# A conditioned decoder layer on one core: the modulation's multiply-adds placed behind later weight splits on VectorE, and the rotary half-swap moved from TensorE to VectorE

## The chip, the core and the metric

One core of one Trainium2 chip runs the whole layer as one program. The metric is the device time of that core in microseconds (us); smaller is better. The engines are named as the profile names them: PE is TensorE, PEld its weight load, DVE is VectorE, ACT is ScalarE, SP is the engine that issues nearly every transfer.

## What is computed

256 tokens of width 2048 pass through one layer and a final norm, all in float32:

```
mods = silu(c) @ ada_w + ada_b          # 9 vectors of 2048: shift, scale and gate of three sublayers
x += 1/2 * gate1 * SwiGLU_1(mod(norm(x)))
x += gate2 * W_out( sig(gA)*UpA(GatedDeltaNet(h)) + sig(gB)*UpB(NSA(h)) ),  h = mod(norm(x))
x += 1/2 * gate3 * SwiGLU_2(mod(norm(x)))
y  = RMSNorm(x)
rope(x) = concat(x1*cos - x2*sin, x2*cos + x1*sin, rest)    # x1, x2: 16 rows each of a head's 128
```

The nine modulation vectors need the whole of `ada_w` (2048 x 18432, 151 MB) for one token's worth of arithmetic. They are products of one row vector, so the kernel does them on DVE as multiply-adds and not on PE.

## The kernel before, in words

**Weights and their split.** Activations lie transposed, 128 channels by 256 tokens a tile. A weight arrives in chunks of 128 x 1024 numbers (512 KB, `raw`, `wload` L157, or `block_load` L329), six buffers in all (`RB = 6`, tag `raw`). ACT rounds a chunk to its high half (`whi`, L171), DVE subtracts to get the low half (`wlo`, L172, or L343 in `block_rows`); three buffers each (`WB = 3`). A buffer of `raw` comes free with the `wlo` that reads it. For every 128 x 128 block `product` (L177) issues a matmul of the high half against 512 columns (high and low half of the activation, L181) and one of the low half against 256 columns (L183). A projection of 2048 inputs is two chunks and 16 such pairs.

**The modulation.** `ada_unit` (L223) handles 256 rows of `ada_w` for 1024 columns: two loads `adaraw` (L230), 512 KB each and from the same six `raw` buffers, and for each a multiply-add on DVE into `acc` (L232 for the first row block, L234 for the rest). After eight units PE transposes `acc` (L240) and DVE sums it into `modc` (L241, L242). `ada(n)` calls the next units between projections, at a pace that `paces` sets: 16 units over the first 22 projections of the first feed-forward block and 32 over the next 42 (L592), then 4 over 27, 20 over 20 and 24 over 36 projections of the mixer (L606), 16 in the second feed-forward block. The 36 last projections of the mixer's paces are the merge gates and the up-projections (L1107 to L1129), the "merge stage" below. The first two modulation vectors are made in `mods` (L421) with loads `sada` (L434) and multiply-adds L441, L443, beside the first gate and up products.

**What sets the order.** A tile framework gives each engine one instruction list. It may reorder what the source has in sequence: an instruction goes into its engine's list when the framework's own estimate says its inputs are there. On the chip each engine takes its list strictly in order. SP's list of loads has the source's order, so numbers of tiles such as `raw_15147` and `adaraw_15238` grow in the order of the transfer queue.

**The rotary swap.** `rope` (L979) copies a 128 x 256 tile, and multiplies the first 32 rows by a constant 32-row matrix `C_ROT` on PE (L982) to exchange the two halves of 16 rows with a sign. DVE multiplies the result, from PSUM, by the sines (L984), the rows themselves by the cosines (L985) and adds (L986). It runs for four key tiles (`attend_in`) and eight query tiles (`soft` in `attend`).

Of the kernel before, what the change touches and what calls it, by code (L numbers as in the profile page):

```python
# [18 lines left out]
F32 = mybir.dt.float32  # L19
# [8 lines left out]
P = 128  # L28
# [33 lines left out]
C_ID, C_ONE, C_TRI, C_UP, C_SUF, C_NEG, C_CAUS, C_ROT = [i * P for i in range(8)]  # L62
C_COS = C_ROT + 32
# [6 lines left out]
def float_consts():  # L70
# [11 lines left out]
    for m in range(16):  # L82
        c[16 + m, C_ROT + m] = -1.0
        c[m, C_ROT + 16 + m] = 1.0
# [5 lines left out]
    c[:16, C_SIN:C_SIN + S] = c[16:32, C_SIN:C_SIN + S] = np.sin(ang)  # L90
# [17 lines left out]
def trunk(tc, a, out, stage=99, dbg=None):  # L108
    nc = tc.nc
    ctx = ExitStack()  # L110
    with ctx:
# [44 lines left out]

        def wload(src, nk):  # L157
            raws = []
            for k0 in range(0, nk, 8):
                n = min(8, nk - k0)  # L160
                raw = wp.tile([P, 8, P], F32, tag="raw", name="raw", bufs=RB)
                nc.sync.dma_start(raw[:, :n], src[:, k0:k0 + n])
                raws.append((raw, n))
            return raws

        def wsplit(raws):
            parts = []
            for raw, n in raws:
# [3 lines left out]
                nc.vector.tensor_sub(lo[:, :n], raw[:, :n], hi[:, :n])  # L172
# [50 lines left out]
        def ada_unit(m, hf, k2, st):  # L223
            if k2 == 0:
                st["acc"] = wp.tile([P, HC], F32, tag="acc", name="acc", bufs=1)
            acc = st["acc"]
            for j in range(2):
                kt = 2 * k2 + j
                raw = wp.tile([P, HC], F32, tag="raw", name="adaraw", bufs=RB)
                nc.sync.dma_start(raw, a["ada_w"][kt * P:(kt + 1) * P, m * D + hf * HC:m * D + (hf + 1) * HC])  # L230
                if kt == 0:
                    nc.vector.tensor_scalar(acc, raw, cact[:, kt:kt + 1], None, op0=OP.mult)  # L232
                else:
                    nc.vector.scalar_tensor_tensor(acc, raw, cact[:, kt:kt + 1], acc, op0=OP.mult, op1=OP.add)  # L234
            if k2 == KT // 2 - 1:
                c0 = hf * 8
                for q in range(2):
                    pt = ftile((P, 4, P))
                    for j in range(4):
# [3 lines left out]
                                     V["ada_b"][:, m * KT + c0:m * KT + c0 + 8])  # L243

# [68 lines left out]
        def gains(A, gain, m_scale, sl):  # L313
            nc.vector.scalar_tensor_tensor(A[:, sl], modc[:, m_scale, sl], 1.0, gain[:, sl], op0=OP.add, op1=OP.mult)
            nc.vector.tensor_scalar(A[:, sl], A[:, sl], RS, None, op0=OP.mult)
# [22 lines left out]
        def block_rows(ps, srcs, hT, k0, kb, first, last):  # L338
# [4 lines left out]
            nc.vector.tensor_sub(lo, raw, hi)  # L343
# [9 lines left out]
        class Entry:  # L353
# [56 lines left out]
        def start(fp, n, sizes, wgu, gain):  # L410
# [9 lines left out]
            with tc.tile_pool(name="sp", bufs=1) as sp:  # L420
                def mods(k0, kb):  # L421
# [10 lines left out]
                    for kt in range(KT):  # L432
# [11 lines left out]
                        yield  # L444
                    sl = slice(k0, k0 + kb)
# [70 lines left out]
        def ffn(fp, wgu, wd, m_gate, ticks, first, post=None):  # L516
            if True:
# [21 lines left out]
                def down(g):  # L539
                    if g == 0:  # L540
                        nc.vector.tensor_scalar(g05, modc[:, m_gate], 0.5, None, op0=OP.mult)
# [62 lines left out]
        with ExitStack() as mx:  # L604
# [386 lines left out]
            def attend_in(g):  # L991
                kk = mp.tile([P, 2, S], F32, tag="kk", name="kk", bufs=2)
                vt = mp.tile([P, 2, 2, P], F32, tag="vt", name="vt", bufs=2)
                for b in range(2):
                    rope(both(win(W_KV + 4 * (b + 1) + g)), kk[:, b], ftile, tmp)
# [35 lines left out]
            def attend(g, kk, vt, qs):  # L1031
# [3 lines left out]
                def soft(r, qt):  # L1035
                    if qt == 0:
                        qr[r] = rope(qs[r], mp.tile([P, S], F32, tag="qr", name="qr", bufs=2), ptile, tmpc)
# [101 lines left out]
        g2 = nrm.tile([P, KT], F32, tag="g05", name="g05", bufs=2)  # L1139
        nc.vector.tensor_scalar(g2, modc[:, 5], 0.5, None, op0=OP.mult)  # L1140
# [100 lines left out]
```

## Time and profile before

| what | before |
|---|---|
| time, median of 3 runs | 2400.68 us (2399.38 to 2405.51) |
| profiled execution: its own time | 2402.11 us |
| profiled execution: span of the trace | 2400.3 us |
| PE busy | 2333.8 us, 97% of the span |
| DVE busy | 1786.4 us, 74% |
| ACT busy | 1130.7 us, 47% |
| moved by DMA | 571 MB, 238 GB/s over the span |
| share of the chain that ended last | PE 79%, DMA 9%, DVE 8% |

The span is counted from the first to the last instruction of the core; the profiled execution's own time is 1.8 us more. A busy time of PE is a model of overlapping matmuls, so the places where PE is idle, and the number of matmuls in equal stretches, say more than its busy share. Most rows of the profile give a line, an engine, an operation, what is written from what is read, a count, and times.

### The profile page before, as it was taken

What the parts mean: (1) busy time and instruction counts of PE and PEld (TensorE: products, weight loads), DVE (VectorE), ACT (ScalarE), POOL (GpSimd) and SP (SyncE); (2) the same over time, 40 slices, a digit from 0 to 9 for tenths busy, and PEclk for the clock granted to TensorE, in tenths of its full rate; (3) what the DMA queues carried; (4) which work ended last, traced back from release to release, by engine and by line L of the source; (5) the groups of instructions that cost most, each with busy time, mean ns of one, the idle gap of its engine ahead of it and who ended that gap; (6) DMA issues with size and microseconds to landing.
All of it is one profiled execution on the core that took longest, in us unless ns stands there. A gap on an engine that the chain in (4) does not pass through costs nothing.

```text
span 2400.3 us, 39307 instructions
## 1 busy us (share of the span) xinstructions
PE 2333.8 (97%) x15310; PEld 2048.3 (85%) x15310; DVE 1786.4 (74%) x2637; ACT 1130.7 (47%) x1784; POOL 1.5 (0%) x8
## 2 busy tenths in 40 slices
PE   6999999999999999999999989999999999999997
PEld 6999978888888988888887878889888888888886
DVE  6899878778887887789886777888666666555555
ACT  3544544334444565554444434556444444344443
POOL 0000000000000000000000000000000000000000
PEclk8999999999999999999999999999999999999999
DMA  9998688888887645558676877666777776665663
GB/s 326 321 318 308 202 280 302 282 279 295 315 306 221 221 164 189 185 178 270 223 241 222 293 266 241 208 229 195 237 239 237 239 239 197 185 191 187 181 185 122
DMA packets 182827, 571.05 MB, mean 238 GB/s; under 512 B 18032, under 2 KB 18288, under 8 KB 182640
## 3 DMA queue, kind: packets, MB, share of 16 engines
q1 hardware_dynamic: 181920, 566.43, 72.2%
q8 instruction: 120, 1.97, 0.3%
q10 hardware_dynamic: 720, 2.11, 0.2%
q14 instruction: 67, 0.55, 0.1%
HBM read 564.27 MB, written 4.19 MB: 237 GB/s over the span
## 4 chain that ended last, share of the span: by engine, by line
PE 79%; DMA 9%; DVE 8%; issue 2%; ACT 1%; DVEq 0%; SPq 0%; ACTq 0%
PE mm L181 41%; PE mm L183 21%; PE mm L348 9%; DMA adaraw<-in_ada_w_dram 8%; DVE wlo L172 3%; PE c L348 2%; DMA sada<-in_ada_w_dram 1%; DVE acc L234 1%; DVE sacc L443 1%; DVE wlo L343 1%; DMA raw<-in_win_dram 0%; PE c L1041 0%; PE f L240 0%; ACT whi L171 0%; PE c L817 0%
## 5 line engine op out<-in xcount | busy, mean ns | idle before, releaser
L181 PE MATMUL mm<-hpair,whi 128*128 128x512 f32 x3536 | 1259.5, 398 | 1.4 <-ACT t L203 1.4
L172 DVE TENSOR_TENSOR wlo<-raw,whi 128x1024 fp32r<-128x1024 f32 (+1 forms) x666 | 792.9, 1196 | 347.0 <-ACT whi L171 345.7
L171 ACT ACTIVATE whi<-raw 128x1024 fp32r<-128x1024 f32 (+1 forms) x666 | 689.8, 1037 | 760.2 <-PE mm L181 449.0
L183 PE MATMUL mm<-hpair,wlo 128*128 128x256 f32 x3536 | 1003.7, 284 | 21.3 <-DVE wlo L172 21.1
L181 PEld LDWEIGHTS mm<-hpair,whi 128*128 128x128 f32 x3536 | 665.1, 188 | 159.4 <-issue 2.8
L183 PEld LDWEIGHTS mm<-hpair,wlo 128*128 128x128 f32 x3536 | 668.3, 189 | 33.3 <-DVE wlo L172 28.1
L181 PE MATMUL mm<-apair,whi 128*128 128x512 f32 x1408 | 498.1, 397 | 0.0
L183 PE MATMUL mm<-apair,wlo 128*128 128x256 f32 x1408 | 397.2, 282 | 3.3 <-DVE wlo L172 3.1
L234 DVE SCALAR_TENSOR_TENSOR acc<-adaraw,cact,acc 128x1024 f32<-128x1024 f32 x210 | 269.0, 1281 | 133.2 <-DMA adaraw<-in_ada_w_dram 132.1
L181 PEld LDWEIGHTS mm<-apair,whi 128*128 128x128 f32 x1408 | 264.3, 188 | 64.6
L183 PEld LDWEIGHTS mm<-apair,wlo 128*128 128x128 f32 x1408 | 265.4, 188 | 5.5 <-DVE wlo L172 5.5
L348 PE MATMUL mm<-hpair,whi 128*128 128x256 f32 x1472 | 265.0, 283 | 2.4 <-ACT hpair L309 1.8
L348 PEld LDWEIGHTS mm<-hpair,whi 128*128 128x128 f32 x1472 | 227.9, 190 | 3.0 <-ACT hpair L309 1.9
L348 PE MATMUL mm<-hpair,wlo 128*128 128x256 f32 x736 | 208.2, 283 | 0.5 <-DVE wlo L343 0.4
L342 ACT ACTIVATE whi<-raw 128x1024 fp32r<-128x1024 f32 x112 | 118.5, 1059 | 144.5 <-DMA raw<-in_w1gu_dram 53.6
L343 DVE TENSOR_TENSOR wlo<-raw,whi 128x1024 fp32r<-128x1024 f32 x112 | 136.4, 1222 | 29.2 <-ACT whi L342 29.0
L348 PEld LDWEIGHTS mm<-hpair,wlo 128*128 128x128 f32 x736 | 139.6, 190 | 1.1 <-DVE wlo L343 1.0
L207 ACT ACTIVATE t<-mm 128x256 f32<-128x256 f32 x237 | 86.4, 366 | 0.1
L210 DVE TENSOR_TENSOR t<-mm,t 128x256 f32<-128x256 f32 x193 | 80.7, 418 | 2.9 <-ACT t L207 2.8
L443 DVE SCALAR_TENSOR_TENSOR sacc<-sada,cact,sacc 128x1024 f32<-128x1024 f32 x57 | 73.0, 1281 | 5.9 <-DMA sada<-in_ada_w_dram 5.5
L532 ACT ACTIVATE t<-t 128x256 f32<-128x256 f32 x63 | 26.3, 418 | 98.4 <-DVE t L210 98.2
L546 DVE SCALAR_TENSOR_TENSOR xT<-mm,g,xT 128x256 f32<-128x256 f32 x128 | 61.7, 482 | 7.7 <-PE mm L183 5.6
(374 smaller groups left out, 1563.5 us busy)
## 6 DMA issues: line engine op xcount, KB each, us to landing
adaraw<-in_ada_w_dram SPq DMA_DIRECT2D x224, 512.0 KB, 5.0
raw<-in_w2gu_dram SPq DMA_DIRECT2D x180, 512.0 KB, 4.7
raw<-in_w1gu_dram SPq DMA_DIRECT2D x176, 512.0 KB, 5.7
raw<-in_win_dram SPq DMA_DIRECT2D x158, 512.0 KB, 5.0
sada<-in_ada_w_dram SPq DMA_DIRECT2D x64, 512.0 KB, 6.1
raw<-in_w1d_dram SPq DMA_DIRECT2D x64, 512.0 KB, 4.6
raw<-in_w2d_dram SPq DMA_DIRECT2D x64, 512.0 KB, 3.6
raw<-in_wup_dram SPq DMA_DIRECT2D x32, 512.0 KB, 4.6
```

The costliest lines, as they stand in the source:

```text
L171: nc.scalar.activation(hi[:, :n], raw[:, :n], AF.Copy)
L172: nc.vector.tensor_sub(lo[:, :n], raw[:, :n], hi[:, :n])
L181: nc.tensor.matmul(ps[:, :], hi, pairs[k][:, :, :].rearrange("p a b -> p (a b)"), start=(k == 0), stop=False, skip_group_check=True)
L183: nc.tensor.matmul(ps[:, S:2 * S], lo, pairs[k][:, 0, :], start=False, stop=(k == n - 1), skip_group_check=True)
L207: nc.scalar.activation(t, ps[:, S:2 * S], AF.Copy)
L210: nc.vector.tensor_add(o, ps[:, :S], t)
L234: nc.vector.scalar_tensor_tensor(acc, raw, cact[:, kt:kt + 1], acc, op0=OP.mult, op1=OP.add)
L342: nc.scalar.activation(hi, raw, AF.Copy)
L343: nc.vector.tensor_sub(lo, raw, hi)
L348: nc.tensor.matmul(ps[:, w], l[:, w, k], h[:, r], start=(first and w == k == x == 0), stop=(last and k == kb - 1 and x == 2), skip_group_c ...
L443: nc.vector.scalar_tensor_tensor(acc, raw, c, acc, op0=OP.mult, op1=OP.add)
L546: nc.vector.scalar_tensor_tensor(xT[:, d], pd[:, j * S:(j + 1) * S], g05[:, d:d + 1], xT[:, d], op0=OP.mult, op1=OP.add)
```

## The change

Two things are changed.

First, the multiply-adds of the modulation are no longer issued where their loads are. `ada_unit` and `mods` put them into a list `late`. Each low-half split (`wlo`, in `wsplit` and `block_rows`) then takes entries out of that list, all but one of them or the only one, and ties each to stand behind this `wlo` in DVE's instruction list. Since the loads of the following projection are issued after the modulation's, such a `wlo` reads a chunk that is later in the transfer queue than the multiply-add's own load. Before a use of the results `flush` empties the list. The loads themselves stay where they were.

Second, `rope` uses DVE's `stream_shuffle` within 32 rows in place of the matmul; the sign goes into the sine constants and the matrix `C_ROT` goes away.

```diff
-    for m in range(16):
-        c[16 + m, C_ROT + m] = -1.0
-        c[m, C_ROT + 16 + m] = 1.0
...
+        late = []
+
+        def behind(ins):
+            for _ in range(max(1, len(late) - 1) if late else 0):
+                with tc.issue_after(ins.ins):
+                    late.pop(0)()
+
+        def flush():
+            while late:
+                late.pop(0)()
...
-                nc.vector.tensor_sub(lo[:, :n], raw[:, :n], hi[:, :n])
+                behind(nc.vector.tensor_sub(lo[:, :n], raw[:, :n], hi[:, :n]))
...
         def ada_unit(m, hf, k2, st):
...
+            for kt in (2 * k2, 2 * k2 + 1):
+                raw = wp.tile([P, HC], F32, tag="raw", name="adaraw", bufs=RB)
+                nc.sync.dma_start(raw, a["ada_w"][kt * P:(kt + 1) * P, m * D + hf * HC:m * D + (hf + 1) * HC])
+                late.append(lambda kt=kt, raw=raw: add(kt, raw))
+            if k2 == KT // 2 - 1:
+                late.append(columns)
...
-            nc.vector.tensor_sub(lo, raw, hi)
+            behind(nc.vector.tensor_sub(lo, raw, hi))
...
                         elif kt == 0:
-                            nc.vector.tensor_scalar(acc, raw, c, None, op0=OP.mult)
+                            late.append(lambda raw=raw, c=c: nc.vector.tensor_scalar(acc, raw, c, None, op0=OP.mult))
                         else:
-                            nc.vector.scalar_tensor_tensor(acc, raw, c, acc, op0=OP.mult, op1=OP.add)
+                            late.append(lambda raw=raw, c=c: nc.vector.scalar_tensor_tensor(
+                                acc, raw, c, acc, op0=OP.mult, op1=OP.add))
+                        if k0 == 0:
+                            flush()
                         yield
+                    flush()
...
-            def rope(x, o, pt, tr):
+            def rope(x, o, tr):
                 nc.scalar.activation(o, x, AF.Copy)
-                pr = pt((P, S))
-                nc.tensor.matmul(pr[:32], cf[:, C_ROT:C_ROT + 32], x, start=True, stop=True)
                 t = tr()
-                nc.vector.tensor_mul(t[:32], pr[:32], cf[:32, C_SIN:C_SIN + S])
+                nc.vector.stream_shuffle(t[:32], x[:32], [(i + 16) % 32 for i in range(32)])
+                nc.vector.tensor_mul(t[:32], t[:32], cf[:32, C_SIN:C_SIN + S])
                 nc.vector.tensor_mul(o[:32], x[:32], cf[:32, C_COS:C_COS + S])
```

`flush()` also stands in `gains`, `shift`, `down(0)` and ahead of `g2`.

**The order on DVE in the merge stage, before.** This is DVE's list around the loads `raw_15145` to `adaraw_15241`; `cat`, `t` and `Dt` belong to the merge arithmetic, `modc` to the end of a modulation vector.

```order
L172 TENSOR_TENSOR wlo_15150<-raw_15145,whi_15149 128x1024
L210 TENSOR_TENSOR cat_14963<-mm_15012,t_15063 128x256
L241 TENSOR_REDUCE modc_77<-f_15091 128x4
L232 TENSOR_SCALAR acc_15237<-adaraw_15238,cact_68 128x1024
L242 TENSOR_TENSOR modc_77<-modc_77,vec_71 128x8
L234 SCALAR_TENSOR_TENSOR acc_15237<-adaraw_15241,cact_68,acc_15237 128x1024
L210 TENSOR_TENSOR t_15117<-mm_15098,t_15115 128x256
L172 TENSOR_TENSOR wlo_15154<-raw_15147,whi_15153 128x1024
L1125 SCALAR_TENSOR_TENSOR Dt_13932<-Dt_13932,t_15117 128x256
L172 TENSOR_TENSOR wlo_15198<-raw_15193,whi_15197 128x1024
```

The multiply-adds of `adaraw_15238` and `adaraw_15241` stand ahead of the splits of `raw_15147` and `raw_15193`, which are earlier in the transfer queue.

**The same place with the change.** The four loads of the merge gates are now `raw_15118` to `raw_15183`, the modulation's pair is `adaraw_15225` and `adaraw_15227`, and `raw_15233`, `raw_15235` are the next up-projection's.

```order
L183 TENSOR_TENSOR wlo_15186<-raw_15181,whi_15185 128x1024
L1148 TENSOR_TENSOR Dt_13917<-Dt_13917 128x256
L250 TENSOR_REDUCE modc_77<-f_15138 128x4
L183 TENSOR_TENSOR wlo_15190<-raw_15183,whi_15189 128x1024
L251 TENSOR_TENSOR modc_77<-modc_77,vec_71 128x8
L183 TENSOR_TENSOR wlo_15238<-raw_15233,whi_15237 128x1024
L221 TENSOR_TENSOR cat_15116<-mm_15117,t_15177 128x256
L238 TENSOR_SCALAR acc_15241<-adaraw_15225,cact_68 128x1024
L183 TENSOR_TENSOR wlo_15244<-raw_15235,whi_15243 128x1024
L241 SCALAR_TENSOR_TENSOR acc_15241<-adaraw_15227,cact_68,acc_15241 128x1024
```

The two multiply-adds moved behind all four earlier chunks and behind one and two chunks that come after them in the queue.

**The rotary swap.** On PE, before, this is the place in the first attention group where a key tile's swap (`f<-t,cf`) and a query tile's (`c<-q,cf`) stand among the matmuls of projections:

```order
L1043 MATMUL c<-cr 128x2x128
L982 MATMUL f<-t,cf 32x256
L183 MATMUL mm<-hpair,wlo 128x256
L181 MATMUL mm<-hpair,whi 128x512
L1065 MATMUL c<-cf,G 128x128 x2
L982 MATMUL c<-q,cf 32x256
L183 MATMUL mm<-hpair,wlo 128x256
```

With the change PE's list has none of the twelve L982, and DVE's has twelve shuffles; here are the first two query tiles' on DVE:

```order
L1005 STREAM_SHUFFLE tc<-q 32x256
L1007 TENSOR_TENSOR qr<-q,cf 32x256
L1006 TENSOR_TENSOR tc<-tc,cf 32x256
L1005 STREAM_SHUFFLE tc<-q 32x256
L1008 TENSOR_TENSOR qr<-qr,tc 32x256
L1006 TENSOR_TENSOR tc<-tc,cf 32x256
L1007 TENSOR_TENSOR qr<-q,cf 32x256
```

Four instructions of DVE per tile stand where there were three.

## Rows read from the trace of the kernel before

**Rows 1.** The page: the chain that ended last, share of the span by engine.
```profile
PE 79%; DMA 9%; DVE 8%; issue 2%; ACT 1%; DVEq 0%; SPq 0%; ACTq 0%
```

**Rows 2.** Stretches: us, busy (count) PE PEld DVE ACT POOL, clock, DMA share, GB/s.
```profile
37.00:300.00 263.00, 260.57 (x2159) 258.80 (x2160) 230.51 (x289) 126.50 (x172) 0.00 (x0) 0.98 0.84 286
300.00:450.00 150.00, 144.15 (x815) 123.75 (x814) 118.10 (x140) 65.42 (x96) 0.00 (x0) 1.00 0.87 292
450.00:600.00 150.00, 145.78 (x824) 125.15 (x823) 116.63 (x132) 57.84 (x65) 0.00 (x0) 1.00 0.86 284
600.00:800.00 200.00, 199.20 (x1131) 172.41 (x1130) 158.76 (x212) 95.15 (x134) 0.00 (x0) 1.00 0.83 280
...
1150.00:1250.00 100.00, 100.00 (x577) 81.84 (x576) 84.63 (x189) 48.85 (x115) 0.00 (x0) 1.00 0.69 224
1250.00:1350.00 100.00, 96.46 (x550) 82.20 (x549) 71.21 (x104) 46.34 (x78) 0.00 (x0) 1.00 0.75 247
1350.00:1450.00 100.00, 90.23 (x498) 76.83 (x497) 71.93 (x86) 41.01 (x56) 0.00 (x0) 0.98 0.80 269
1450.00:1500.00 50.00, 47.66 (x271) 40.93 (x271) 37.05 (x52) 23.27 (x37) 0.00 (x0) 1.00 0.75 242
...
1650.00:2380.00 730.00, 730.00 (x4199) 637.19 (x4198) 454.30 (x574) 345.35 (x480) 0.00 (x0) 1.00 0.66 206
```

**Rows 3.** Waits: who waited for whom, us in total, times, longest us.
```profile
DVE acc L234 <- DMA adaraw<-in_ada_w_dram: 132.1, 90, 4.5
...
PE mm L183 <- DVE wlo L172: 24.3, 25, 2.2
```

**Rows 4.** One stall, by engine: start us, us, engine, line, what [idle before].
```profile
1396.00 0.68 DVE L241 TENSOR_REDUCE modc<-f 128x4 f32<-128x512 f32 x1
1400.56 0.75 DVE L232 TENSOR_SCALAR acc<-adaraw,cact 128x1024 f32<-128x1024 f32 x1 [3.88 <-DMA adaraw<-in_ada_w_dram]
...
1403.35 1.22 DVE L172 TENSOR_TENSOR wlo<-raw,whi 128x1024 fp32r<-128x1024 f32 x1
...
1399.98 1.06 ACT L171 ACTIVATE whi<-raw 128x1024 fp32r<-128x1024 f32 x1 [1.48 <-issue]
...
1404.62 0.38 PE L183 MATMUL mm<-hpair,wlo 128*128 128x256 f32 x1 [1.54 <-DVE wlo L172]
```

**Rows 5.** SP's issues there: start of first, us to end of last, count.
```profile
1392.95 1.43 SPq L230 DMA_DIRECT2D adaraw<-in_ada_w_dram  x2
1395.78 5.89 SPq L162 DMA_DIRECT2D raw<-in_wup_dram  x2
```

**Rows 6.** The tile adaraw, issue to landing; the page's median landing of sada.
```profile
DMA to landing us min/median/max: 3.4/5.0/7.7
...
sada<-in_ada_w_dram SPq DMA_DIRECT2D x64, 512.0 KB, 6.1
```

**Rows 7.** Groups by line: count | busy us, mean ns | idle before, releaser.
```profile
L172 DVE TENSOR_TENSOR wlo<-raw,whi 128x1024 fp32r<-128x1024 f32 (+1 forms) x666 | 792.9, 1196 | 347.0 <-ACT whi L171 345.7
L171 ACT ACTIVATE whi<-raw 128x1024 fp32r<-128x1024 f32 (+1 forms) x666 | 689.8, 1037 | 760.2 <-PE mm L181 449.0
...
L234 DVE SCALAR_TENSOR_TENSOR acc<-adaraw,cact,acc 128x1024 f32<-128x1024 f32 x210 | 269.0, 1281 | 133.2 <-DMA adaraw<-in_ada_w_dram 132.1
...
L210 DVE TENSOR_TENSOR t<-mm,t 128x256 f32<-128x256 f32 x193 | 80.7, 418 | 2.9 <-ACT t L207 2.8
```

**Rows 8.** PE's list in time at one swap; L982 appears as two rows.
```profile
1157.64 0.62 PE L982 MATMUL c<-q,cf 128*32 128x256 f32 x2
1158.19 0.50 PE L181 MATMUL mm<-hpair,whi 128*128 128x512 f32 x1
```

**Rows 9.** Groups by line, nearest prices for a shuffle.
```profile
L798 DVE STREAM_TRANSPOSE tb<-zc 128x128 f32<-128x128 f32 x20 | 6.1, 306 | 0.3
...
L985 DVE TENSOR_TENSOR qr<-q,cf 32x256 f32<-32x256 f32 x8 | 3.2, 406 | 0.0
...
L896 DVE TENSOR_TENSOR o<-o,roy 128x512 f32<-128x512 f32 x4 | 2.7, 685 | 0.1
```

More of the change, by code (lines that the diff above doesn't have):

```diff
@@ L59 @@
 ROPE_DIM = 32
-C_ID, C_ONE, C_TRI, C_UP, C_SUF, C_NEG, C_CAUS, C_ROT = [i * P for i in range(8)]
-C_COS = C_ROT + 32
+C_ID, C_ONE, C_TRI, C_UP, C_SUF, C_NEG, C_CAUS = [i * P for i in range(7)]
+C_COS = C_CAUS + P
 C_SIN = C_COS + S
@@ L89, in float_consts @@
     c[:16, C_COS:C_COS + S] = c[16:32, C_COS:C_COS + S] = np.cos(ang)
-    c[:16, C_SIN:C_SIN + S] = c[16:32, C_SIN:C_SIN + S] = np.sin(ang)
+    c[16:32, C_SIN:C_SIN + S] = np.sin(ang)
+    c[:16, C_SIN:C_SIN + S] = -c[16:32, C_SIN:C_SIN + S]
     for qt in range(2):
@@ L223, in ada_unit, with add, columns @@
         def ada_unit(m, hf, k2, st):
[L224 to L230, printed above, removed]
+            def add(kt, raw):
                 if kt == 0:
-                    nc.vector.tensor_scalar(acc, raw, cact[:, kt:kt + 1], None, op0=OP.mult)
+                    st["acc"] = wp.tile([P, HC], F32, tag="acc", name="acc", bufs=1)
+                    nc.vector.tensor_scalar(st["acc"], raw, cact[:, kt:kt + 1], None, op0=OP.mult)
                 else:
+                    acc = st["acc"]
                     nc.vector.scalar_tensor_tensor(acc, raw, cact[:, kt:kt + 1], acc, op0=OP.mult, op1=OP.add)
-            if k2 == KT // 2 - 1:
+            def columns():
+                acc = st["acc"]
                 c0 = hf * 8
@@ L440, in mods @@
                         elif kt == 0:
-                            nc.vector.tensor_scalar(acc, raw, c, None, op0=OP.mult)
+                            late.append(lambda raw=raw, c=c: nc.vector.tensor_scalar(acc, raw, c, None, op0=OP.mult))
                         else:
-                            nc.vector.scalar_tensor_tensor(acc, raw, c, acc, op0=OP.mult, op1=OP.add)
+                            late.append(lambda raw=raw, c=c: nc.vector.scalar_tensor_tensor(
+                                acc, raw, c, acc, op0=OP.mult, op1=OP.add))
+                        if k0 == 0:
+                            flush()
                         yield
+                    flush()
                     sl = slice(k0, k0 + kb)
@@ L540, in down @@
                     if g == 0:
+                        flush()
                         nc.vector.tensor_scalar(g05, modc[:, m_gate], 0.5, None, op0=OP.mult)
@@ L994, in attend_in @@
                 for b in range(2):
-                    rope(both(win(W_KV + 4 * (b + 1) + g)), kk[:, b], ftile, tmp)
+                    rope(both(win(W_KV + 4 * (b + 1) + g)), kk[:, b], tmp)
                     v = both(win(W_KV + 4 * (b + 1) + 2 + g))
@@ L1036, in soft @@
                     if qt == 0:
-                        qr[r] = rope(qs[r], mp.tile([P, S], F32, tag="qr", name="qr", bufs=2), ptile, tmpc)
+                        qr[r] = rope(qs[r], mp.tile([P, S], F32, tag="qr", name="qr", bufs=2), tmpc)
                     n = (qt + 1) * P
@@ L1139, in trunk @@
         g2 = nrm.tile([P, KT], F32, tag="g05", name="g05", bufs=2)
+        flush()
         nc.vector.tensor_scalar(g2, modc[:, 5], 0.5, None, op0=OP.mult)
```

## The prediction

> **What bounds the kernel now.** I read the chain that ended last first. PE holds 79% of it, transfers 9% and DVE 8% [rows 1], so the kernel is PE's, with a fringe where PE waits for something that DVE and the transfer queue hand on. To see where that fringe lies I cut the span into stretches [rows 2]. From 1650 to 2380 us PE is never idle, and 730 us for 4199 matmuls is 0.174 us a matmul; a projection of 2048 inputs, 32 matmuls, costs 5.56 us at that pace. PE falls behind in two places. Between 300 and 800 us its idle time is 5.85 + 4.22 + 0.80 = 10.9 us, between 1250 and 1500 us it is 3.54 + 9.77 + 2.34 = 15.7 us. These are the stretches in which the modulation's loads run beside projections; where they are rare the idle time is gone.
>
> The table of waits names the link: PE waited 24.3 us in 25 places for a low half, and DVE waited 132.1 us in 90 places with a multiply-add at the head of its list for that multiply-add's load [rows 3]. One stall shows how the two hang together [rows 4]. DVE has nothing it may do from 1396.7 us on, because `adaraw` stands next in its list; that load lands only at 1400.5 us. ACT finished the high half of an earlier chunk at 1399.98 + 1.06 = 1401.04 us, but its low half waits behind two multiply-adds and starts at 1403.35 us, and PE stands idle until 1404.62 us. The stalled load itself was issued late [rows 5], and the second load of the next pair was issued when the first multiply-add was over (1400.56 + 0.75 = 1401.31 us; the issue ends at 1401.67 us, 0.4 us later): a buffer ring that is held up by its own newest loads.
>
> **The multiply-adds.** Their number and length don't change: 210 of 1.28 us and 14 short ones, on DVE, which has room. What changes is their place. By the list of before, 201 of the 224 stand ahead of one to five splits of chunks that are earlier in the queue; by the new list 222 stand behind every earlier chunk, and 221 behind one or two later ones as well. The loads keep their order on SP, so no transfer is moved past another, but the moment of each issue moves, since a buffer is released by another instruction.
>
> In the built programs I counted, for the merge stage, how many loads earlier the releasing instruction's own load is. Before: for 20 of 37 issues that wait for a multiply-add it is three loads, and for those that wait for a split six to ten. With the change: four to six for a split, seven or eight for a multiply-add. So the short loop of before is landing, multiply-add 1.28 us [rows 7], 0.4 us to the next issue: with the median landing of 5.0 us [rows 6] 6.7 us for three loads, 2.2 us a load. What PE asks for in the merge stage is 120 loads (48 + 72) for 36 projections, 120 in 36 x 5.56 = 200 us, 1.67 us a load. Three such loops stand for about ten loads, 20.1 us, where three projections take 16.7.
>
> The tight loop of the change is longer but spans more: issue, landing, high half 1.04, low half 1.20, an add 0.42, multiply-add 1.28, low half 1.20, multiply-add 1.28 [rows 7], 0.4 to the issue: landing + 6.8 us for six loads. The other four loads of three projections go at DVE's own pace, two splits, two multiply-adds and two adds, 5.8 us. Together landing + 12.6 us for ten loads: 17.6 us at a landing of 5.0 us, 16.6 us at 4.0 us, against PE's 16.7.
>
> How much of the 24.3 us goes follows from where that lies. The loop of before overstates: it gives 2.01 us a load at 5.0 us, while the stretch itself ran at 1.67 x 250 / 234.3 = 1.78 us. Scaled by the same factor the new loop gives 1.56 us, faster than PE, and all 24.3 us go; taken at face value it gives 1.76 us, and nothing goes. Those are the two ends. I take 70%, 17 us, nearer the first, because the new loop holds a landing once in ten loads and the old one three times, and because releases that alternate between splits and multiply-adds should spread the issues, which shortens the landing towards its shortest, 3.4 us [rows 6].
>
> The Trainium skill (DMA: Bandwidth & Descriptors, Anatomy of one DMA) puts one DMA at about 2.0 us plus its bytes over 436 GB/s, measured on the other issue path; that is an estimate of 3.2 us for 512 KB. The shortest landing in the trace, 3.4 us, agrees; the median does not, since loads queue behind each other. By the page's figure the new loop would take 15.8 us for ten loads and every wait would go.
>
> **The rotary swap.** Twelve matmuls of PE go, each two rows in the profile. From the start of such a pair to the start of the next matmul it is 1158.19 - 1157.64 = 0.55 us [rows 8], 6.6 us in all, in a part where PE is never idle (1150 to 1250 us, 100.00 of 100 us [rows 2]). On DVE twelve shuffles of 32 x 256 come in. No row has one: the nearest are 0.31 us for a transposing stream of 128 elements, 0.41 us for a two-operand product of this very tile, and 0.69 us for 512 elements [rows 9]. I take the row of this tile, 0.41 us, 4.9 us in all, between 3.7 and 8.2. They lie beside PE's work, but DVE is 84.6% busy there [rows 2]; with 4.9 us more in a stretch 6.6 us shorter it is at 96%, little cover. So I book 5 us of the 6.6, with 0 and 6.6 as ends.
>
> The Trainium skill (VectorE: DVE Perf Modes, The perf-mode tier table) gives the shuffle one element a cycle and no faster mode, about 2400 ns for 2048 elements. An estimate from that page, 150 cycles and 256 cycles at 0.96 GHz, is 0.42 us, or 5.1 us for twelve; no run here shows it.
>
> **The sum.** The profiled execution took 2402.1 us. Less 17 and 5 it is 2380.1; it lay 1.4 us above the median of the runs, so against the median I expect **2379 us**.
>
> **Rivals.**
>
> *Every wait goes.* By the scaled loop PE would never wait in these stretches and the swap would save its full 6.6 us: 2402.1 - 24.3 - 6.6 - 1.4 = 2370 us. For it speaks that from 600 to 800 us, at 280 GB/s, PE lost only 0.8 us [rows 2]. Against it: some places need ten loads in less than the loop's time. Chance 0.13.
>
> *The transfers are the limit.* At full pace the first feed-forward block's gate and up projections ask for 3.52 loads in 5.56 us, 332 GB/s; 292 GB/s went with a DMA share of 0.87 [rows 2], which is 336 at a full share. If that can't be reached nothing is won before 800 us: 2402.1 - 0.7 x 15.7 - 5 - 1.4 = 2385 us. Chance 0.07.
>
> *The wait changes its name.* A low half now waits for its own chunk, whose load is issued four to six loads after the one that releases its buffer, where it was six to ten. At face value the loop is as slow as now, and only the swap pays: 2402.1 - 5 - 1.4 = 2396 us. Chance 0.15, one third of it below 2393.5.
>
> *Slower: the first 300 us starve.* There the change touches a stretch in which PE loses only 263 - 260.6 = 2.4 us [rows 2]. A `raw` load's issue waits for a split five loads earlier (38 of 51), before six or seven. PE's 24 matmuls per chunk take 2.92 us (263 us / 2159 x 24) and ask for 1.9 loads, 1.54 us a load. The loop is landing 6.1 us [rows 6], 1.04 + 1.20 [rows 7] and 0.4: 8.7 us for five loads, 1.75 us. Over some 114 loads that is 0.21 x 114 = 24 us. If the later waits stay too, the time is 2402.1 + 24 - 5 - 1.4 = 2420 us. It decides from a landing above 5 x 1.54 - 2.64 = 5.1 us on. Against it: 6.1 us is the landing with more loads in flight, and a shorter ring shortens it. Chance 0.10.
>
> **How the numbers follow.** A measurement of this kernel can tell about 0.3%, 7 us, from no change: faster is below 2393.5, slower above 2407.9. The forecast, with 2372 to 2388 around it, has the 0.55 that is left. Faster: 0.55 + 0.13 + 0.07 + 0.05 = 0.80; same 0.10; slower 0.10. The range of 2368 to 2397 takes in all cases but the slower one and leaves out a little at either edge of the others, together under 0.2; it spans the two ends of both unknown costs.
>
> **What would show it.** In the changed profile DVE's wait for `adaraw` (132.1 us) should nearly vanish and its wait for the high half grow; PE's wait for the low half should fall from 24.3 to about 7 us; the stretch of the merge gates should lose its 15.7 us of idle time. L982 is gone, and twelve shuffles of about 0.4 us stand on DVE with PE still fully busy around them. The forecast is wrong if PE's wait for the low half stays over 15 us, if PE shows new idle time before 300 us, or if PE waits for query tiles in the attention.

## Result and profile after

| | before | change |
|---|---|---|
| time, median of the undisturbed runs | 2401.89 us (2399.38 to 2405.51) | 2424.44 us (2418.93 to 2434.23) |
| ratio, 95% interval | | 1.0099 [1.0074, 1.0123] |
| profiled execution: span, own time | 2400.3, 2402.11 us | 2422.6, 2424.44 us |
| PE busy, idle | 2333.8, 66.5 us | 2333.6, 89.0 us |

The change is 1% slower; 2379 us, 2368 to 2397, had been forecast. (A fourth run of the change, at a granted clock of 0.653, took 3224 us and is left out; with it the median is 2429 us, the number that the expectations below use.)

The chain that ended last has less of PE than in [rows 1], and its transfers are no longer `adaraw` (8% of the span on the page of before) but weight chunks:

```profile
PE 67%; DMA 15%; DVE 9%; ACT 4%; issue 3%; ACTq 0%; DVEq 0%; SPq 0%
PE mm L192 38%; PE mm L194 19%; DMA raw<-in_w1gu_dram 9%; PE mm L365 5%; DMA raw<-in_win_dram 4%; DVE wlo L183 3%; ACT whi L182 3%; PE c L365 1%; DVE acc L241 1%; DMA raw<-in_wup_dram 1%; DVE sacc L461 1%; DVE wlo L360 1%; ACT whi L359 1%; DMA raw<-in_w1d_dram 1%; PE f L249 1%
```

The table of waits, all engines (us in total, times, longest us):

```profile
DVE wlo L183 <- ACT whi L182: 494.0, 417, 3.7
...
ACT whi L182 <- DMA raw<-in_w1gu_dram: 100.7, 49, 4.2
ACT whi L182 <- DMA raw<-in_win_dram: 88.8, 49, 4.8
...
PE f L249 <- DVE acc L241: 24.6, 10, 4.5
...
PE mm L194 <- DVE wlo L183: 11.2, 21, 0.8
...
DVE acc L241 <- DMA adaraw<-in_ada_w_dram: 0.6, 1, 0.6
```

What the change was to take away is gone: DVE's 132.1 us for `adaraw` [rows 3] are 0.6, PE's 24.3 us for the low half 11.2. Two waits have come in their place. ACT now waits for weight chunks to land, and PE's transposes of `acc` (L249) wait for the multiply-adds that were put off.

The stretches of [rows 2] again (columns as there):

```profile
37.00:300.00 263.00, 255.08 (x2102) 251.55 (x2103) 223.85 (x279) 121.20 (x164) 0.00 (x0) 0.99 0.83 277
300.00:450.00 150.00, 142.03 (x801) 121.75 (x800) 115.12 (x139) 65.77 (x98) 0.00 (x0) 0.99 0.84 280
450.00:600.00 150.00, 147.33 (x834) 127.10 (x833) 112.52 (x129) 57.51 (x63) 0.00 (x0) 1.00 0.85 281
600.00:800.00 200.00, 189.93 (x1063) 163.16 (x1062) 154.16 (x198) 88.11 (x124) 0.00 (x0) 0.98 0.82 269
...
1150.00:1250.00 100.00, 94.94 (x564) 81.01 (x565) 89.22 (x196) 49.60 (x109) 0.00 (x0) 1.00 0.71 235
1250.00:1350.00 100.00, 96.63 (x554) 82.51 (x553) 76.69 (x140) 48.30 (x95) 0.00 (x0) 0.98 0.73 237
1350.00:1450.00 100.00, 93.02 (x513) 80.66 (x514) 72.19 (x87) 42.05 (x58) 0.00 (x0) 0.96 0.82 272
1450.00:1500.00 50.00, 47.30 (x268) 40.62 (x266) 36.60 (x44) 19.72 (x28) 0.00 (x0) 1.00 0.83 274
1500.00:1650.00 150.00, 146.50 (x821) 127.59 (x822) 119.53 (x197) 77.46 (x120) 0.00 (x0) 0.98 0.66 217
```

PE's idle time against before: 5.5 us more ahead of 300 us, 0.6 more from 300 to 600, 9.3 more from 600 to 800 (10.1 where it was 0.8), 5.1 more from 1150 to 1250, 2.6 less from 1250 to 1500 and 3.4 more from 1500 to 1650. Where PE used to wait little changed; the new idle time is in stretches that had had little or none.

The same work falls into different windows in the two kernels, so here is where the time went by the moments at which SP issues the first load of a stage (us between them):

| from, to | before | change |
|---|---|---|
| start, first `adaraw` | 287.2 | 295.2 |
| first `adaraw`, first `win` (rest of the first feed-forward block) | 477.4 | 492.6 |
| first `win`, first `wup` (mixer) | 592.1 | 600.7 |
| first `wup`, first `wout` (up-projections of the merge stage) | 169.6 | 165.7 |
| first `wout`, end of the span | 874.0 | 868.4 |

The change is 8.0 + 15.2 + 8.6 = 31.8 us behind when the up-projections begin. In the merge stage, which was read for the forecast, it is the faster one. (A load is issued ahead of PE's use by a lead that varies, so a few us can move between neighbouring rows.)

One piece of the chain, in the merge stage (start us, us, what):

```profile
1473.82 5.21 DMA raw<-in_win_dram
...
1483.70 1.24 DVE wlo L183
1484.96 5.79 DMA raw<-in_wup_dram
1490.85 1.07 ACT whi L182
1491.94 0.45 DVE wlo L183
...
1493.19 4.77 DMA raw<-in_win_dram
...
1502.25 1.20 DVE acc L241
1503.50 1.11 PE f L249 x4
1504.61 0.43 PE mm L192
1505.04 0.21 PE mm L194
...
1509.15 0.23 PE mm L192
1509.38 0.12 PE mm L194
```

A chunk lands, ACT rounds it, DVE splits it, that (or a multiply-add right behind it) releases a buffer, SP issues the next load into it, and so round again; from 1473.82 us until the end of PE's stall at 1503.50 us the chain has no matmul. (From 640 to 700 us, in the first feed-forward block, the chain goes round in the same way.) SP's issues in the same stretch tell how many loads one turn carries (start of the first, us to the end of the last, count):

```profile
1455.44 4.19 SPq L173 DMA_DIRECT2D raw<-in_win_dram  x4
1461.83 1.85 SPq L256 DMA_DIRECT2D adaraw<-in_ada_w_dram  x2
1465.83 1.53 SPq L173 DMA_DIRECT2D raw<-in_wup_dram  x2
1468.53 2.23 SPq L256 DMA_DIRECT2D adaraw<-in_ada_w_dram  x2
1473.82 4.19 SPq L173 DMA_DIRECT2D raw<-in_win_dram  x4
1481.48 1.86 SPq L256 DMA_DIRECT2D adaraw<-in_ada_w_dram  x2
1484.96 1.52 SPq L173 DMA_DIRECT2D raw<-in_wup_dram  x2
1487.66 2.23 SPq L256 DMA_DIRECT2D adaraw<-in_ada_w_dram  x2
1493.19 4.30 SPq L173 DMA_DIRECT2D raw<-in_win_dram  x4
```

From 1465.83 to 1473.82 us four loads go out in 7.99 us, from 1484.96 to 1493.19 four in 8.23 us; in between come six, in 10.4 and 11.1 us. Twenty loads take 1493.19 - 1455.44 = 37.75 us, 18.9 us for ten, and every turn, the long and the short, holds a landing. PE asks for ten loads in 16.7 us.

The theory that the experiments test (A, held buffers): a multiply-add that stands behind a later chunk's split holds its `raw` buffer until that later chunk has been loaded, rounded and split. With six buffers the load that reuses this buffer is then only four or five places behind the later chunk's in the queue, and the ring falls behind PE. Rivals: the order on DVE as such costs (B); the late sums block PE's own list through the transposes (C); the number of buffers in play on the mean decides (D).

### The profile page after: what moved, and what is told of

Its sections match the earlier page's. It is cut to its first block, busy times and chain, and to the rows that moved or that the text cites. A ratio compares the mean times of both kernels' runs of the same rounds, so it can differ in the third digit from the quotient of the medians.

```text
span 2422.6 us, 39318 instructions
## 1 busy us (share of the span) xinstructions
PE 2333.6 (96%) x15286; PEld 2052.5 (85%) x15286; DVE 1791.1 (74%) x2661; ACT 1130.4 (47%) x1784; POOL 1.5 (0%) x8
## 4 chain that ended last, share of the span: by engine, by line
PE 67%; DMA 15%; DVE 9%; ACT 4%; issue 3%; ACTq 0%; DVEq 0%; SPq 0%
PE mm L192 38%; PE mm L194 19%; DMA raw<-in_w1gu_dram 9%; PE mm L365 5%; DMA raw<-in_win_dram 4%; DVE wlo L183 3%; ACT whi L182 3%; PE c L365 1%; DVE acc L241 1%; DMA raw<-in_wup_dram 1%; DVE sacc L461 1%; DVE wlo L360 1%; ACT whi L359 1%; DMA raw<-in_w1d_dram 1%; PE f L249 1%
## 5 line engine op out<-in xcount | busy, mean ns | idle before, releaser
L183 DVE TENSOR_TENSOR wlo<-raw,whi 128x1024 fp32r<-128x1024 f32 (+1 forms) x666 | 796.9, 1197 | 494.7 <-ACT whi L182 494.0
L194 PE MATMUL mm<-hpair,wlo 128*128 128x256 f32 x3536 | 1005.6, 285 | 10.7 <-DVE wlo L183 10.5
L194 PEld LDWEIGHTS mm<-hpair,wlo 128*128 128x128 f32 x3536 | 670.4, 190 | 20.6 <-DVE wlo L183 18.7
L218 ACT ACTIVATE t<-mm 128x256 f32<-128x256 f32 x237 | 86.3, 366 | 10.7 <-PE mm L194 10.7
```

What stands on the lines that cost most here:

```text
L183: behind(nc.vector.tensor_sub(lo[:, :n], raw[:, :n], hi[:, :n]))
L194: nc.tensor.matmul(ps[:, S:2 * S], lo, pairs[k][:, 0, :], start=False, stop=(k == n - 1), skip_group_check=True)
L218: nc.scalar.activation(t, ps[:, S:2 * S], AF.Copy)
```

## The experiments

Each ratio is to the kernel before, run on the same chip. "Places" is counted in the built programs, for loads of the merge stage that wait for DVE (106 to 127, by kernel): how many loads earlier in the queue is the newest one that the releasing instruction, or any ahead of it on DVE, reads. The last column is the time from the first `wup` load to the first `wout` load, as in the table of stretches.

| kernel | median us | ratio [95%] | issues by places | `wup` to `wout`, us |
|---|---|---|---|---|
| before, 6 buffers | 2402 | 1 | 1 to 3: 20, 4: 24, 5: 25, 6: 51 | 169.6 |
| change, 6 | 2424 | 1.0099 [1.0074, 1.0123] | 4: 30, 5: 52, 6: 44 | 165.7 |
| one later chunk, 6 | 2430 | 1.0116 [1.0087, 1.0145] | 4: 28, 5: 45, 6: 54 | 157.2 |
| queue order, 6 | 2371 | 0.9863 [0.9833, 0.9893] | 5: 5, 6: 107 | 153.6 |
| before, 7 | 2386 | 0.9924 [0.9899, 0.9949] | 2, 3: 14, 4: 16, 5: 27, 6: 23, 7: 40 | 162.7 |
| change, 7 | 2368 | 0.9857 [0.9835, 0.9879] | 5: 21, 6: 53, 7: 45 | 149.0 |
| queue order, 7 | 2366 | 0.9848 [0.9827, 0.9868] | 6: 3, 7: 103 | 151.3 |
| queue order, 5 | 2398 | 0.9987 [0.9977, 0.9998] | 4: 6, 5: 114 | 155.4 |
| change, 5 | 2554 | 1.0625 [1.0608, 1.0643] | 3: 27, 4: 51, 5: 44 | 177.6 |

Within the merge stage the kernels with many short leads are the slow ones, before among them. Over the whole kernel the count does not rank before against the change: before has the shorter leads and is 22 us faster. It is so ahead of the merge stage too: between the first `adaraw` load and the last `w1gu` load 34 issues of before have two or three places, and none of the change has fewer than four, yet there the change lost time to before. The loops hold different work (in before often a multiply-add's own load, in the change a chunk's load, its rounding and its split); why the change's cost more there is not shown.

**The shuffle alone.** The multiply-adds stay where they were.

```diff
-                late.append(lambda kt=kt, raw=raw: add(kt, raw))
+                add(kt, raw)
...
```

> The rotary swap on VectorE alone; the multiply-adds are issued where they were before. Theory of the split list (the loss comes from the multiply-adds' new place): 5 us faster than before, about 2396 us, PE still 100% busy around the attention. Rival (the shuffles load VectorE so that the attention starves PE): 2400 us or more, with PE idle 3 to 5 us between 1150 and 1250 us.

2391.7 us, 0.9952 [0.9935, 0.9969]: 10 us faster, more than the 6.6 us that the matmuls took. PE's wait for the low half is as before (23.6 us). PE's busy time fell by 7.2 us (2333.8 to 2326.6), near those 6.6, and its idle time by 3.0 in all: 5.0 less from 1250 to 1500 us (15.7 to 10.7) and 2.1 more from 300 to 600.

**The late order alone.** The change with the matmul put back into `rope`.

```diff
-                nc.vector.stream_shuffle(t[:32], x[:32], [(i + 16) % 32 for i in range(32)])
+                nc.tensor.matmul(pr[:32], cf[:, C_ROT:C_ROT + 32], x, start=True, stop=True)
...
```

> The multiply-adds placed as in the change, the rotary swap by the matmul as before. Theory of the split list: 27 to 35 us slower than before, about 2430 us, since the change lost 27 us with a gain of some 5 in it. Rival (the shuffles cost): nearer to before than the change is, 2405 to 2415 us.

2438.0 us, 1.0149 [1.0117, 1.0181]. So the whole loss is the order's: 36 us, of which the swap gives back some 13.5 in the change (the intervals of the two just overlap).

**The transposes out of the way.** The change, but the transposes of `acc` go into a list of their own and are tied on PE behind the last matmul of a projection.

```diff
+            if cols and not late:
+                with tc.issue_after(last.ins):
+                    cols.pop(0)()
...
-                late.append(columns)
+                cols.append(columns)
...
```

> The change, but the transposes of acc that end a modulation vector are tied on PE behind the last matmul of the next projection once its multiply-adds are out. Theory that PE's own list blocks (transposes stand where acc is not yet done, 24.6 us of PE waits): these waits fall under 5 us and the time falls by 15 to 25 us, to about 2405 us. Rival theory of held buffers (the waits of PE are only where the lateness of the chunks shows): the waits for transposes go, waits for low halves take their place, and the time stays within 6 us of the change.

2422.5 us, 1.0079 [1.0052, 1.0106]; its interval overlaps the change's. PE's waits at the transposes, in the table of waits:

```profile
PE f L255 <- DVE modc L256: 6.8, 9, 1.7
...
PE f L255 <- DVE acc L247: 2.3, 1, 2.3
```

The 24.6 us at `acc` are nearly gone (6.8 + 2.3 us are left at the transposes) and the time has hardly moved, while ACT waits longer than in the change for landings (w1gu 112.3 us, win 96.5 us). The wait at the transposes was where PE stood while the ring was behind, not why it was. That speaks against C.

**Exact queue order.** Each multiply-add is tied behind the last `wlo` that has already been emitted, so it stands behind every chunk that is ahead of its load in the queue and behind none that follows.

```diff
...
         def behind(ins):
-            for _ in range(max(1, len(late) - 1) if late else 0):
-                with tc.issue_after(ins.ins):
-                    late.pop(0)()
+            split_[:] = [ins]
+
+        def tied(f):
+            if split_:
+                with tc.issue_after(split_[0].ins):
+                    f()
+            else:
+                f()
...
-                late.append(lambda kt=kt, raw=raw: add(kt, raw))
+                tied(lambda kt=kt, raw=raw: add(kt, raw))
...
```

> The multiply-adds stand in VectorE's list exactly in the order of the transfer queue: behind every chunk issued earlier, ahead of every chunk issued later; shuffles as in the change. Theory of held buffers: an accumulator's buffer is free as soon as its own load is in, so this loses neither to newer loads (as before did) nor to later chunks (as the change does): 10 to 20 us faster than before, 2380 to 2390 us. Rival (the order on VectorE doesn't matter, the transfer engines are full): between before and the change, 2400 to 2415 us.

2370.9 us, 0.9863 [0.9833, 0.9893]: it beats both kernels, by more than theory A had expected. In its stretches (here two of them) PE's idle time is all but gone, 0.4 us from 300 to 800 and 0.7 from 1250 to 1500; from 800 to 1250 us it is longer than in before, 15.1 against 7.2 us:

```profile
600.00:800.00 200.00, 200.00 (x1141) 174.11 (x1140) 157.10 (x211) 96.53 (x133) 0.00 (x0) 1.00 0.82 277
...
1350.00:1450.00 100.00, 99.36 (x569) 86.12 (x568) 87.09 (x105) 45.56 (x64) 0.00 (x0) 1.00 0.89 309
```

and SP's issues go at PE's pace:

```profile
1400.96 4.74 SPq L180 DMA_DIRECT2D raw<-in_win_dram  x4
1406.56 1.65 SPq L263 DMA_DIRECT2D adaraw<-in_ada_w_dram  x2
1409.38 2.30 SPq L180 DMA_DIRECT2D raw<-in_wup_dram  x2
1413.83 3.16 SPq L263 DMA_DIRECT2D adaraw<-in_ada_w_dram  x2
1417.86 4.73 SPq L180 DMA_DIRECT2D raw<-in_win_dram  x4
```

Ten loads in 1417.86 - 1400.96 = 16.90 us, against 18.9 with the change. PE waits 0.6 of 100 us at 309 GB/s, so the transfers are not the limit there. By the stretches between first loads (287.0, 463.4, 590.4, 153.6, 875.4 us) it saves against the change 8.2 us at the start, 29.2 in the rest of the first feed-forward block, 10.3 in the mixer and 12.1 in the up-projections, and the last stretch takes 7.0 us more.

**One later chunk.** A split takes all waiting multiply-adds, so none stands behind two later chunks.

```diff
-            for _ in range(max(1, len(late) - 1) if late else 0):
+            for _ in range(len(late)):
```

> The change, except that a low-half split takes every waiting multiply-add behind it, so that none stands behind more than one later chunk (the change: one, or two for the second of a pair). Theory A (a multiply-add behind later chunks holds its raw buffer until those have landed and been split, so the ring of six is short): the cost goes with the number of later chunks, the time lies about half way between exact queue order, 2371 us, and the change, 2429 us: 2390 to 2410 us, and ACT's waits for chunks to land lie between those of the two. Rival B (being behind any later chunk is what costs, since the multiply-add then waits for a load of its own future): within 8 us of the change, 2421 us or more. Rival C (the late sums that PE's transposes wait for): PE's wait for acc falls by about half from 24.6 us and the time by no more than 12 us, 2415 to 2425 us.

2430.2 us: nothing gained. By theory A's size this is a miss, and rival B's number. The count of places says why it can't tell the two apart: 28 issues at four places and 45 at five, where the change has 30 and 52; by the count it is mostly the first later chunk that shortens a lead. The total hides two things, though. The up-projections took 157.2 us against the change's 165.7 and 153.6 in queue order, more than half way, as A had it for the whole. The mixer took 612.2 us against 600.7; there the granted clock was 0.84 from 1150 to 1175 and 0.80 from 1200 to 1225 us, where the change has 1.00, after 5.0 us of idle PE from 1100 to 1150 (3.3 in the change). The rest of the first feed-forward block stayed as it was, 492.0 against 492.6 us.

**Seven buffers for the change.** The room comes from the second buffer of the attention's `pT`, which is given up in all three kernels with seven; that edit was not tried alone. (In queue order it and the seventh buffer together moved the time by only 5 us, see below.)

```diff
-RB = 6
+RB = 7
...
-                        pT[r] = mp.tile([P, 2, 3, P], F32, tag="pT", name="pT", bufs=2)
+                        pT[r] = mp.tile([P, 2, 3, P], F32, tag="pT", name="pT", bufs=1)
```

> The change with seven raw buffers in place of six (room from the second buffer of the attention's transposed weights pT, which is done in all three kernels with seven). Theory A (held buffers): one more buffer gives back what one later chunk holds, so the time falls by 20 to 40 us to 2390 to 2410 us, ACT's waits for landings (w1gu 100.7, win 88.8 us) fall by half or more. Rival B or C (the order on DVE and PE's list themselves, whatever the number of buffers): less than 8 us gained, 2421 us or more, PE's wait for acc still over 20 us.

2368.4 us, 56 us under the change with six, and more than A had expected. The list on DVE is still the change's, each multiply-add behind later splits. The waits that had come are gone (table of waits, as above):

```profile
ACT whi L182 <- DMA raw<-in_w1gu_dram: 27.0, 11, 3.9
...
ACT whi L182 <- DMA raw<-in_win_dram: 20.7, 12, 3.0
...
PE f L249 <- DVE acc L241: 3.1, 4, 1.3
```

That rules out B: the order as such costs nothing that can be told from noise once the ring has room for what it holds (2368.4 against 2366.2 us in queue order, below).

**Seven buffers for the kernel before**, the same edit on it.

> The kernel before with the same seventh buffer. In its own short loop of three loads a buffer makes four of three, so theory A expects a gain here too, but a smaller one than the change has: 5 to 15 us, 2387 to 2397 us, PE's wait for the low half from 24.3 to 10 to 18 us; the distance between change and before falls from 27 us to 15 or less. Under rivals B and C the distance stays over 20 us.

2386.4 us: 15 to 19 us gained, at the upper edge or over, PE's wait for the low half 15.0 us. The change gained three times as much and is now 18 us faster than before, where it was 22 us slower; some of the 18 is the shuffle's.

**Seven buffers in queue order**, the same edit again.

> Exact queue order with the same seventh buffer. Theory A: its ring is hardly short, PE waits 4.3 us for low halves in all, so no more than 5 us is left: 2366 to 2372 us. A rival by which transfers land late whatever the ring would show here as no change of the time and of the landing times; a gain of over 8 us would mean that six buffers still cost time that PE's waits don't show.

2366.2 us, 0.9848 [0.9827, 0.9868], the fastest; its interval overlaps those of the change with seven and of queue order with six. As expected, little was left.

**Five buffers in queue order.** `RB = 5`, nothing else.

> Exact queue order with five raw buffers: nearly every load's issue then hangs on work for the load five places ahead of it in the queue (counted in the built program: 114 of 120 in the merge stage; the change with six: 30 at four places, 52 at five, 44 at six). Theory A, in the form that the shortest of these loops sets the pace: landing 5.4 + high half 1.04 + low half 1.20 + 0.4 to the issue is 8.0 us for five loads, 1.61 us a load, where the merge stage asks for 1.67 and the first feed-forward block for 1.58: little is lost there, some 5 to 10 us in the first 300 us, where 1.54 is asked: 2375 to 2395 us, well under the change although the mean number of places (4.95) is under the change's (5.11). Rival D (the mean number of places, or buffers in all, decides, and not the few shortest loops): over 2430 us.

2398.3 us, 3 us over A's range and 32 under D's bound. With fewer buffers and a lower mean of places (4.95 against 5.11) it beats the change with six by 26 us. So neither the mean nor the number of buffers decides between these two; it speaks for the few loads with a short lead (30 issues at four places in the change, 6 here). Of the 20.6 us between its profiled span and that of six buffers 9.1 are lost before the first `adaraw` load, as A had it, 6.2 in the rest of the first feed-forward block and 5.9 in the mixer, where A had counted on little. The sum of A took the median landing; a longer one costs at once where 1.61 us a load stand against 1.54 to 1.67, which may be why.

**Five buffers for the change.** `RB = 5`.

> The change with five raw buffers: 27 of 122 issues of the merge stage then hang on work for the load three places ahead, a multiply-add included. Theory A: from seven to six buffers it lost 61 us, and the loops shorten from four places to three: a further 80 us or more, over 2510 us, with PE idle in every stretch that has modulation loads. Rival B or C (order on DVE, late sums on PE): about as far from exact queue order with five buffers as with six, 60 us.

2553.5 us, 129 us over the change with six and 155 over queue order with five. PE's wait at `acc` is 0.4 us in this run, so C, by which that wait is the loss, is out too. From 600 to 800 us PE is idle for 23.2 us, where queue order with five loses 4.4.

**Only the start late.** Exact queue order, but `sada` in `mods` goes behind later splits as in the change.

```diff
             split_[:] = [ins]
+            for _ in range(max(1, len(late) - 1) if late else 0):
+                with tc.issue_after(ins.ins):
+                    late.pop(0)()
...
-                            tied(lambda raw=raw, c=c: nc.vector.tensor_scalar(acc, raw, c, None, op0=OP.mult))
+                            late.append(lambda raw=raw, c=c: nc.vector.tensor_scalar(acc, raw, c, None, op0=OP.mult))
...
```

> Exact queue order everywhere, but the first two modulation vectors (loads sada, before 300 us) placed behind later splits as in the change. It measures what the late order costs in the first 300 us. Theory A: 34 of 98 issues go from six places to five; the change's stretch from 37 to 300 us had 5.6 us less PE work than exact queue order, so 2374 to 2379 us. The rival of the prediction (the first 300 us starve) by its own sum: 24 us, 2395 us.

2379.8 us, 9 us over exact queue order, just over A's range. PE did 2088 matmuls from 37 to 300 us, 71 fewer than the 2159 of queue order; at 263 / 2159 = 0.122 us each that is 8.7 us. The rival's mechanism is there at a third of its price.

**Queue order with the matmul swap.** `rope` as in the second experiment.

> Exact queue order with the rotary swap as a matmul on PE again, as before. Without the waits of the merge stage the swap's worth is seen by itself: if it is the twelve matmuls that PE no longer has, 6.6 us, the time is 2377 to 2378 us; if the 10 us of the shuffle alone (2392 against 2402 us) were all the swap's own, 2381 us; if DVE's shuffles delay PE in the attention, where exact queue order has 12 us of idle time against 7 before, less than 3 us are lost: 2371 to 2374 us.

2373.6 us, 0.9883 [0.9868, 0.9898]: the shuffle is worth 2.7 us here, not clear of noise, since the interval overlaps that of queue order with the shuffle. The stretch of the attention, in this kernel and then in queue order with the shuffle:

```profile
1150.00:1250.00 100.00, 99.94 (x580) 81.60 (x579) 85.96 (x203) 50.68 (x125) 0.00 (x0) 1.00 0.66 217
```

```profile
1150.00:1250.00 100.00, 97.05 (x572) 82.16 (x571) 91.41 (x223) 53.37 (x131) 0.00 (x0) 1.00 0.66 225
```

With the multiply-adds behind earlier splits and twelve shuffles more, DVE is 91% busy and PE idles for 3 us where it had idled for none.

## Why the prediction was wrong

*What bounds the kernel, and the waits that would go.* Right: `adaraw` at the head of DVE's list, the low half behind it, a ring held up by its newest loads. Exact queue order removes just that, and with the swap the time falls by 31 us; of the 24.3 us for low halves there is left:

```profile
PE mm L201 <- DVE wlo L190: 4.3, 4, 2.1
```

*The loop of the change: the step that failed.* "The other four loads of three projections go at DVE's own pace, two splits, two multiply-adds and two adds, 5.8 us." They don't. Those four hang on a landing as well: 7.99 and 8.23 us in the chain and SP's issues. Ten loads thus hold two landings and take 18.9 us, not landing + 12.6 = 17.6, although the six took less than the working has (10.4 and 11.1 us where landing + 6.8 is 11.8); PE's pace is 16.7, which queue order keeps to (16.90). So in the up-projections of the merge stage, the stage on which the 17 us were worked out, the change gained 3.9 us. I had counted whose instruction releases a buffer and how old that one's own load is, "seven or eight" loads for a multiply-add. What counts is the newest load that anything ahead of it on DVE's list must have: four to six.

*The term that the sum does not have.* The sum books gains alone; new idle time where PE had hardly waited stands at nothing in it, and only a rival priced the first 300 us. That is where the change lost: 8.0 us up to the first `adaraw` load, 15.2 in the rest of the first feed-forward block, 8.6 in the mixer. From 600 to 800 us, which the prediction read as a sign that every wait could go (0.8 us idle), PE idled for 10.1 us. A seventh buffer gives this back with the order kept: 284.1, 466.1 and 591.4 us for the three stretches where the change took 295.2, 492.6 and 600.7. So the ring is what was lost there, too; why it loses more there than the ring of before is open.

*The scaling.* "Scaled by the same factor the new loop gives 1.56 us", faster than PE. The factor, 1.78 / 2.01 = 0.89, came from dividing the mean pace of a stretch in which before was in that loop only part of the time by the loop's pace. In the loop before's face value held. From the first of these rows of SP in that trace to the second go fifty loads:

```profile
1364.76 7.21 SPq L162 DMA_DIRECT2D raw<-in_win_dram  x4
...
1464.23 6.62 SPq L162 DMA_DIRECT2D raw<-in_win_dram  x4
```

That is 19.9 us for ten (18.5 to 20.8 in the single turns), where the working has 20.1. Unscaled, even 17.6 would have said slower than PE.

*The 70%.* One reason was that "releases that alternate between splits and multiply-adds should spread the issues, which shortens the landing". The landing of `adaraw` in the change (issue to landing), to set against [rows 6]:

```profile
DMA to landing us min/median/max: 3.4/5.0/7.5
```

It is the same. The estimate by the Trainium skill (DMA: Bandwidth & Descriptors, Anatomy of one DMA), 3.2 us for 512 KB and with it every wait gone, is met by the shortest landing alone.

*The slower rival.* It had the right sign and kind of cause, a `raw` issue that hangs on a younger split, and 2420 us is near the 2424 measured, but by luck, from another sum: the start costs 8 or 9 us and not 24, and the rest is lost between 290 and 1390 us, which the rival's sum leaves as it was. A chance of 0.10 was too low because I applied the argument to one stretch only.

*The swap.* Shuffles on DVE, in the view of the tile that they write:

```profile
L1005 DVE STREAM_SHUFFLE tc<-q x8: 429/434/435, 1179.5 to 1281.0; 32x256 f32<-32x256 f32 x8
```

434 ns where I took 410. The estimate from the Trainium skill (VectorE: DVE Perf Modes, The perf-mode tier table), 0.42 us, agrees within 4%. Booked were 5 us between 0 and 6.6: 10 were gained beside before's order, some 13.5 beside the late order, 2.7 in queue order. PE's busy time shows the swap's own part in the first and the last: 7.2 us less (2333.8 to 2326.6) and 7.4 less (2330.2 to 2322.8). The rest is idle time, 3.0 us less beside before's order (66.5 to 63.5) and 5.5 more in queue order (41.5 to 47.0). "Little cover" was right for the last; why idle time fell in the first stays open.

*Its own signs.* As foreseen, DVE's wait for `adaraw` vanished, its wait for the high half grew (345.7 [rows 7] to 494.0 us) and PE's for the low half fell, to 11.2 us. But from 1250 to 1500 us 13.1 of the 15.7 us of idle time stayed, and the new idle time before 300 us came that was to say that the forecast is wrong.

*Not foreseen.* The transposes of `acc` wait in PE's list in the change: 24.6 us. The third experiment shows that they cost little beyond what the ring costs anyway.

Settled by the runs: the loss goes with the late order, and a seventh buffer removes it with that order kept. Open: why the change's ring loses more than that of before ahead of the merge stage. Not tried: the second `pT` buffer given up by itself, and a ring of their own for the modulation's loads.

## What to carry to other kernels

When several kinds of work share one ring of buffers, ask of every issue: what is the newest load that must have landed before the instruction that frees this buffer can run, counting all that stands ahead of it on its engine? Landing plus the work behind it, divided by the number of loads between them, is the pace of that loop, and a few short loops can cost more than the mean tells (five buffers in queue order against six in the change). The number of loads alone is not enough: before has the shortest leads and loses less than the change. Ask it in every stage, also where the engine that bounds the kernel has not waited so far. Consume in the order in which the loads are queued, neither earlier (the engine waits at a landing) nor later (the buffer waits for a stranger's landing); and to see whether a loss is the ring's, give it one buffer more or less in both kernels.

## What the runs showed of the hardware

A stall can cost more than its length. In the piece of the chain above PE had been idle for 4.46 us up to 1503.50 us; from 1504.61 us a pair of matmuls takes 0.43 + 0.21 us, from 1509.15 us on 0.23 + 0.12 us. The stretches show the granted clock. First PE's list, then two stretches:

```profile
1503.50 1.11 PE L249 MATMUL f<-cf,acc 128*128 128x128 f32 x4 [4.46 <-DVE acc L241]
```

```profile
1500.00:1510.00 10.00, 6.50 (x26) 5.79 (x27) 8.34 (x13) 3.25 (x6) 0.00 (x0) 0.66 0.86 299
1510.00:1520.00 10.00, 10.00 (x59) 8.73 (x58) 6.67 (x12) 6.32 (x12) 0.00 (x0) 1.00 0.49 162
```

0.66 on average while it goes from its lower level, 1.2 GHz, back to 2.4. For the same 15286 matmuls PE was busy 2322.8 us in queue order (idle 47.0), 2333.6 us in the change (idle 89.0) and 2395.3 us in the change with five buffers (idle 163.6). The third is clear: 72.5 us more of busy time than in queue order, beside 116.6 us more of idle time. Of the 52.8 us of span between the first two 10.8 are busy time, but that much moves without idle time as well: the change with seven buffers was busy for 2311.7 us and idle for 52.9. The prediction priced a wait at its length.

The landing of a 512 KB load hardly depends on how the ring is run: medians of 4.8 to 5.3 us for `adaraw` with five to seven buffers and in every order, while the time went from 2366 to 2554 us.
